# A hybrid decoder trunk: the dilated mixer's second score product on all 128 rows of the array

## The chip, the cores and the metric

One NeuronCore of a Trainium2 chip runs the whole program. The metric is the time on the device of one execution, in microseconds (us), as the median of the runs.

## What is computed

Two layers of a decoder over 1024 tokens of 1024 columns. Each layer projects the tokens to the inputs of four causal mixers of four heads each (A: differential attention, B: spatial gating, C: a dilated mixture, D: an mLSTM), projects the four outputs back, adds and normalizes, and ends with a gated feed-forward. The change is in mixer C. The reference takes three attentions with the same q, k and v, that differ in the keys that a query may see, and mixes them by their softmax sums:

```
def dilated_mixture(q, k, v):
    outs, lses = [], []
    for window, dilation in DILATED_PATTERNS:
        o, l = dilated_pattern(q, k, v, window, dilation)
...
    wts = jax.nn.softmax(jnp.stack(lses, 0), axis=0)
```

This is one softmax over all earlier keys, with a mask that counts by how many of the three patterns a key is seen, and the kernel computes it so: scores q·k over 64 columns a head, plus the mask, exponential, sum, and a product with the values.

## The kernel before

**Split numbers.** The products of the projections and of the scores take operands of the type fp32r, which holds a part of an fp32 number. So each operand is a high part, rounded to fp32r, and a low part, the rest. A projection adds three products (high·high, high·low, low·high) into one PSUM bank (`proj_tok`).

**The stacks of mixer C** (`stacks`, kind "C"). A head has 64 columns, the array of TensorE 128 rows. Per pair of heads, q and k are transposed and written into the arena RA from column `R_ST` on. For q, one block of 512 columns a head: rows 0 to 63 hold q's high part, rows 64 to 127 its low part. For k, two blocks of 1024 columns a head: the first has k's high part in rows 0 to 63 (ScalarE, L415) and again in rows 64 to 127 (GpSimd, `dup`, L421); the second has k's low part in rows 0 to 63 (VectorE, L416), and its rows 64 to 127 are not used.

**The scores** (`attn_S`). A tile is 128 queries of one head, numbered i = 0 to 7; it needs i+1 blocks of 128 keys, in one chunk of keys for i below 4 and in two above. For each chunk a first product of all 128 rows gives q-high·k-high + q-low·k-high, and a second one, of 64 rows, adds q-high·k-low:

```
self.mm(bank[:, 0:wm], self.r(q, 128), self.r(kk + c0, wm), True, False)
self.mm(bank[:, 0:wm], self.r(q, 128, 0, 64), self.r(kk + 1024 + c0, wm, 0, 64), False, True)
```

Chunks have 256, 384 or 512 columns. Four heads of twelve chunks make 48 second products a layer, 96 in the program. VectorE then adds the mask and takes the extreme (L512), ScalarE the exponential (L517).

**The order on TensorE** is the order in which the program is written. `step` interleaves, by the strings `C1` (i below 4) and `C2` of `ORDER`, the scores of this tile (S, one chunk each), the transposes of the weights of the tile two steps earlier (T), their product with the values (P), the end of an earlier pair of tiles (t), and pieces of a queue of projections (- and .), which `Fill` hands out:

```
'C1': 'TT.S-.PP-t', 'C2': 'STT-S--PP-t'
```

So the second product is followed at once by two transposes in the first chunk of tiles 4 to 7 (16 a layer, 32 in all), and by a projection's product otherwise (64 in all). P waits for ScalarE's copy of the transposed weights out of PSUM (`attn_T`, L229). Between a pair's stacks and its first scores some 9 us of projections are issued (`STACK`). The other engines' instructions are ordered by a scheduler. GpSimd computes, in its own order, the low parts of the projections' weights (L256), the copies of k's high part (L421), and small steps of the norms.

**The same arena holds mixer A's stacks** before: four blocks of 1024 columns for k and four of 512 for q, with 96 rows each. Mixer C's low parts lie where A's second and fourth block of keys were.

Of the kernel before, what the change touches and what calls it, by code (L numbers as in the profile page):

```python
# [9 lines left out]
F32 = mybir.dt.float32  # L10
# [5 lines left out]
S = 1024  # L16
D = 1024
# [8 lines left out]
# fp32r arena, in floats per partition  # L26
R_T = 0
R_W = 16384
R_ST = R_W + 6144
R_SIZE = 28672  # L30
# fp32 arena
# [18 lines left out]
# the last slot of q|k is followed by room for the mLSTM values' window of 128 columns  # L50
# [3 lines left out]
# flexible area: fp32 while the mixers run  # L54
# [10 lines left out]
# mLSTM, after the attentions  # L65
# [5 lines left out]
# slots of the weights: 0..5 and 16..23 in the fp32r arena, 6.. in tiles of their own  # L71
DOWN_SLOTS = [[0, 1, 2, 3, 4, 5, 16, 17], [18, 19, 20, 21, 22, 23, 6, 7], [2, 3, 4, 5, 6, 7]]
# where the seven left factors of the Strassen-Winograd products live in the fp32r arena
# [10 lines left out]
# steps of the attention. S: scores of a chunk of keys, T: transposition, P: product with the values,  # L84
# t: end of a pair of tiles, - and .: products from the queue
# [16 lines left out]
class Fill:  # L102
    """a queue of products that are issued between the steps of a chain of dependent work"""
# [28 lines left out]
def blend(a, start, b, every):  # L132
    """work a, with a piece of b after every few of its pieces from a given one on"""
    for i, d in enumerate(a):
        yield d
        if i >= start and (i - start) % every == 0:
            yield next(b, 0.0)
    yield from b


class Trunk:
# [119 lines left out]
    def wplan(self, units):  # L261
        """the weights of the mixers in the order of their use, through three slots"""
        self.wq = collections.deque(units)
        self.wready = collections.deque()
        self.wslots = collections.deque()
# [11 lines left out]
    def rstd(self, out, var, n):  # L277
        """out = (var + eps) ** -0.5 on [128, n]"""
        nc = self.nc
        nc.gpsimd.tensor_scalar(out, var, EPS, 1.0, ALU.add, ALU.mult)  # L280
        nc.gpsimd.tensor_tensor(out, out, self.f(C_MH, 1).to_broadcast([128, n]), ALU.pow)

# [1 line left out]
    def make_T(self, t, src):  # L284
        """src [128 tokens, 1024] fp32 of token tile t into the T ring."""
        h, c = divmod(t, 4)
        for g in range(2):
            bank = self.tr_bank()
            b3 = bank.rearrange("p (k n) -> p k n", k=4)
            for k in range(4):  # L290
                self.tp(b3[:, k, :], src[:, (4 * g + k) * 128:(4 * g + k + 1) * 128])
            self.split(self.th(h)[:, 4 * g:4 * g + 4, c * 128:(c + 1) * 128],
                       self.tl(h)[:, 4 * g:4 * g + 4, c * 128:(c + 1) * 128], b3)

    def behind(self, ins, other):
        """issue order on an engine: ins after other"""
        self.tc.add_manual_dep(ins.ins, other.ins.name,
                               mybir.DependencyInfo(mybir.DependencyClass.NoSync, mybir.DependencyReason.DATA),
                               reason="later")

# [1 line left out]
    def proj_tok(self, kss, n, evac, per_bank=2):  # L302
        """z[:, cols] in token layout. kss: the k blocks of each weight unit; evac(t, bank)"""
        units = []
        for ks in kss:
            hi, lo, slot = self.wready.popleft()
            hi, lo = (w[:, 0:len(ks) * n].rearrange("p (k n) -> p k n", k=len(ks)) for w in (hi, lo))
            units.append((hi, lo, slot, ks))
        for t0 in range(0, 8, per_bank):
            bank = self.mm_bank()  # L310
            for tt in range(per_bank):
                t = t0 + tt
                h, c = divmod(t, 4)
                out = bank[:, tt * n:(tt + 1) * n]
                for hi, lo, slot, ks in units:
                    for i, k in enumerate(ks):
                        xh = self.th(h)[:, k, c * 128:(c + 1) * 128]
                        xl = self.tl(h)[:, k, c * 128:(c + 1) * 128]
                        self.mm(out, xh, hi[:, i, :], k == 0, False)
                        yield n * MM  # L320
                        self.mm(out, xh, lo[:, i, :], False, False)
                        yield n * MM
                        self.mm(out, xl, hi[:, i, :], False, k == 7)
                        if k == 7 and tt == per_bank - 1:
                            evac(t0, bank)
                        if t == 7 and i == len(ks) - 1:
                            self.wdone(slot)
                        yield n * MM
# [4 lines left out]
    def proj_qk(self, slot, ng, hd, cos_off):  # L333
        """q|k of two heads with rope; ng groups of hd columns; half = hd // 8"""
        nc = self.nc
# [22 lines left out]
    def proj_v(self, v):  # L358
        """v: [128, 8 tiles, 256] fp32"""

        def evac(t0, bank):
            self.copy(v[:, t0:t0 + 2, :], bank.rearrange("p (t c) -> p t c", t=2))
            self.vdone = t0 + 2

        return self.proj256(evac)

# [1 line left out]
    def stacks_A(self, src, dst, lo_first, late):  # L368
        """src: callable tile -> [128, 128] (4 maps x 32) ; dst: list of 4 [96, 512] stacks"""
# [19 lines left out]
    def stacks(self, kind, slot, what, half, late=False):  # L389
        """q or k of two heads, transposed, hi and lo parts stacked along the contraction"""  # L390
# [35 lines left out]
    def attention(self, kind, v, col0, slots, marks):  # L426
        """all four heads; marks: what to do at the start of a pair of heads, before a given step"""
        self.steps = 0
        for hp in range(2):
# [45 lines left out]
    def attn_S(self, T):  # L475
# [20 lines left out]
        for m in range(nmap):  # L496
            for ci, (c0, wd) in enumerate(chunks):
# [6 lines left out]
                else:  # L504
# [3 lines left out]
                    self.mm(bank[:, 0:wm], self.r(q, 128, 0, 64), self.r(kk + 1024 + c0, wm, 0, 64), False, True)  # L508
# [18 lines left out]
    def attn_T(self, T):  # L527
        """the weights, transposed"""
# [13 lines left out]
    def attn_PV(self, T):  # L542
        """even key blocks into the rows 0..63, odd ones into 64..127; two query tiles to a bank"""
# [49 lines left out]
    def norm_A(self):  # L593
        """RMS norm of A's outputs, per head"""
# [67 lines left out]
    def proj_dqk(self, l):  # L662
        """q and k: transposed projection, causal depthwise convolution, 2 * silu"""
# [35 lines left out]
    def proj_do(self):  # L699
        """tanh of half the output gate"""  # L700
        ot = self.x(X_OT, 2048).rearrange("p (n c) -> p n c", n=8)
        self.gated = 0

        def evac(t0, bank):
            self.nc.scalar.activation(ot[:, t0:t0 + 2], bank.rearrange("p (t c) -> p t c", t=2), AF.Tanh, scale=0.5)
            self.gated = t0 + 2

        return self.proj256(evac)

    def proj_dv(self):  # L710
        """values and gates of the mLSTM"""
# [13 lines left out]
    def gates_D(self, l):  # L725
        """the gates' logs, running maxima and factors"""
# [42 lines left out]
        # running maximum over the chunks, on one partition  # L769
# [29 lines left out]
        # rows to all partitions through DRAM  # L799
# [11 lines left out]
    def mixer_D2(self, l, c):  # L811
        """recurrence over the chunks; a generator that leaves the tensor engine to other work"""
# [95 lines left out]
    def D_out(self, n0, H):  # L908
        """LayerNorm over the 64 columns of each head, output gate; H [128, 2, 4, 64]"""
# [25 lines left out]
    def make_T_pair(self, t0, ks):  # L935
        """two k blocks of two adjacent token tiles into the T ring"""
# [10 lines left out]
    def mixed_T(self):  # L947
        """outputs of A, B and C, from DRAM, transposed"""
# [40 lines left out]
    def out_part(self, tt, units, ks):  # L989
        """512 columns of a token tile; units: weights of two k blocks each, from block ks[0]"""  # L990
# [11 lines left out]
    def out_A(self, xsrc):  # L1002
        """first half of the columns; A, B and C of six tiles, before the mLSTM ends"""
# [12 lines left out]
    def out_B(self, xsrc, unit):  # L1016
        """the rest of the first half of the columns"""
# [19 lines left out]
    def out_C(self, l):  # L1037
        """second half, first norm (its gain and bias join in after the transposition), start of gate and up"""
# [27 lines left out]
        # the first products, which need the first half of the tokens only, while the last tiles are made  # L1066
# [16 lines left out]
    def form(self, tt):  # L1083
        """left factors of a token tile; those that take both halves of the tokens, after its second tile"""
# [3 lines left out]
        # tiles that have been transposed, or staging, hold what is being mixed  # L1088
# [41 lines left out]
    # ---- feed-forward: gate and up, by Strassen-Winograd over token halves, halves of the contraction  # L1130
    # and gate|up ----
# [11 lines left out]
    def f1_head(self, l, i):  # L1143
        """the right factors of the first two products of tile i"""
# [8 lines left out]
    def f1_prep(self, l, i):  # L1153
        """the right factors of tile i"""
# [70 lines left out]
    def f1_last(self, i):  # L1225
        """the same in an order that frees the mixed left factors first"""
# [352 lines left out]
```

## Time and profile before

| | |
|---|---|
| median of 3 runs | 2654.44 us (2653.58 to 2655.23) |
| span of the profiled execution | 2633.2 us, from its first to its last instruction |
| around the span (launch and end), median less span | 21.2 us |
| TensorE's products, share of the span | 97% |
| weight loads of TensorE | 80% |
| VectorE, ScalarE, GpSimd | 61%, 38%, 18% |
| mean granted clock of TensorE | 0.992 |
| mixer C, layer 1 and layer 2 | about 206 to 360 us and 1512 to 1666 us |

The profile gives the profiled execution by its span alone; the table's third line is worked out with the median of the runs, and so is not known for that one execution. A product on TensorE is a weight load (PEld) and a MATMUL (PE); a row such as `64*128 64x512` means 64 rows by 128 columns of the array in use, and 512 columns streamed through it. Ends of products are modelled, starts are measured. Times on the right of a bar are the idle time of the engine just before, with what ended it.

### The profile page before, as it was taken

The numbers are of one execution on the slowest core, as the hardware profiler recorded it, in microseconds if no ns is written. First come the engines' busy times: TensorE is split into PE (matmuls) and PEld (weight loads), VectorE is DVE, ScalarE is ACT, GpSimd is POOL, SyncE is SP. The second block draws the span as 40 slices with busy tenths as digits, with TensorE's granted clock in tenths as the row PEclk, the third lists the DMA queues.
The fourth block names the chain that finished last, engine by engine and source line by source line (L and its number), as shares of the span: only waits on it lengthen the run. The fifth ranks groups of instructions, "written<-read, shape, count | busy, mean of one in ns | idle before, by whom it ended". The sixth has DMA issues, their size and how long they took to land. (4 is left out here: it accounts for less than half of the span.)

```text
span 2633.2 us, 36905 instructions
## 1 busy us (share of the span) xinstructions
PE 2560.7 (97%) x14128; PEld 2110.0 (80%) x14128; DVE 1601.7 (61%) x3219; ACT 1004.0 (38%) x1918; POOL 484.7 (18%) x478
## 2 busy tenths in 40 slices
PE   8999998998999999999999999989989999999998
PEld 8988886776888888788899878877868888887886
DVE  4775346768766665632756743467687666656336
ACT  4675553226333333211246755522353333322110
POOL 2214122115000000600221231211230000007002
PEclk9999999999999999999999999999999999999999
DMA  4112112412222222532321111132122222235322
GB/s 159 50 36 68 35 34 79 141 54 104 105 80 76 84 81 87 176 120 68 116 76 52 46 56 34 55 121 89 66 103 93 84 80 76 85 104 176 96 84 76
DMA packets 120673, 224.24 MB, mean 85 GB/s; under 512 B 16816, under 2 KB 67888, under 8 KB 120496
## 3 DMA queue, kind: packets, MB, share of 16 engines
q1 hardware_dynamic: 107792, 179.93, 20.9%
q0 software_dynamic: 12704, 41.95, 4.2%
q8 instruction: 111, 1.82, 0.3%
q14 instruction: 66, 0.54, 0.1%
HBM read 167.77 MB, written 46.20 MB: 81 GB/s over the span
## 5 line engine op out<-in xcount | busy, mean ns | idle before, releaser
L222 PE MATMUL bank<-RA 128*128 128x256 f32 (+7 forms) x5016 | 851.6, 317 | 13.8 <-ACT XA L229 9.7
L222 PE MATMUL bank<-RA,wb 128*128 128x512 f32 x3600 | 845.6, 397 | 11.0 <-ACT wb L234 7.4
L222 PEld LDWEIGHTS bank<-RA,wb 128*128 128x128 f32 x3600 | 679.4, 189 | 177.2 <-ACT wb L234 8.3
L222 PEld LDWEIGHTS bank<-RA 128*128 128x128 f32 (+2 forms) x5016 | 696.4, 192 | 107.3 <-issue 44.6
L222 PE MATMUL bank<-RA,h 128*128 128x512 f32 x1728 | 412.8, 396 | 6.3 <-DVE RA L235 5.7
L222 PEld LDWEIGHTS bank<-RA,h 128*128 128x128 f32 x1728 | 323.3, 188 | 87.1 <-DVE RA L235 7.5
L234 ACT ACTIVATE wb<-FA 128x512 fp32r<-128x512 f32 x300 | 189.2, 635 | 500.0 <-PE bank L222 480.3
L235 DVE TENSOR_TENSOR wb<-FA,wb 128x512 fp32r<-128x512 f32 x300 | 208.4, 699 | 5.5 <-ACT wb L234 3.4
L256 POOL TENSOR_TENSOR RA<-FA,RA 128x512 fp32r<-128x512 f32 (+2 forms) x112 | 145.5, 1318 | 325.3 <-ACT RA L255 317.5
L512 DVE CUSTOM_DVE_ANT_0 XA<-bank,XA 128x384 f32<-128x384 f32 (+2 forms) x192 | 109.7, 572 | 128.2 <-PE bank L222 126.6
L517 ACT ACTIVATE XA<-XA,FA 128x128 f32<-128x128 f32 (+3 forms) x192 | 148.4, 773 | 55.3 <-DVE FA L512 54.2
L235 DVE TENSOR_TENSOR RA<-FA,RA 128x1024 fp32r<-128x1024 f32 (+2 forms) x64 | 92.6, 1464 | 95.0 <-ACT RA L234 93.9
L1221 POOL DMA_DIRECT2D hid<-FA x44 | 23.8, 541 | 671.9 <-DVE FA L1212 640.5
L1322 DVE TENSOR_TENSOR FA<-FA,bank 128x512 f32<-128x512 f32 x96 | 64.2, 684 | 136.7 <-PE bank L222 136.7
L234 ACT ACTIVATE RA<-FA 128x512 fp32r<-128x512 f32 (+2 forms) x96 | 78.3, 826 | 168.6 <-DMA FA<-in_w_down 119.6
L225 PE MATMUL bank<-FA,XA 128*128 128x128 f32 (+2 forms) x824 | 128.4, 274 | 6.2 <-DVE XA L929 3.2
L229 ACT ACTIVATE XA<-bank 128x512 f32<-128x512 f32 (+5 forms) x228 | 103.6, 484 | 79.7 <-PE bank L225 66.2
L225 PEld LDWEIGHTS bank<-FA,XA 128*128 128x128 f32 (+2 forms) x824 | 91.4, 140 | 32.8 <-issue 7.8
L234 ACT ACTIVATE h<-FA 128x1024 fp32r<-128x1024 f32 (+1 forms) x48 | 46.9, 988 | 172.1 <-PE bank L222 144.0
L280 POOL TENSOR_SCALAR FA<-FA 128x1 f32<-128x1 f32 (+1 forms) x48 | 17.9, 372 | 504.4 <-DVE FA L976 350.7
L222 PE MATMUL bank<-wx,RA 128*128 128x512 f32 x384 | 97.7, 406 | 0.0
L222 PE MATMUL bank<-XA 128*64 128x128 f32 (+1 forms) x836 | 92.2, 291 | 3.4 <-DVE XA L749 2.5
(187 smaller groups left out, 2647.8 us busy)
## 6 DMA issues: line engine op xcount, KB each, us to landing
FA<-in_w_in SPq DMA_DIRECT2D x44, 512.0 KB, 3.7
FA<-in_w_gate SPq DMA_DIRECT2D x44, 512.0 KB, 3.3
FA<-in_w_up SPq DMA_DIRECT2D x44, 512.0 KB, 3.2
hid<-FA POOLq DMA_DIRECT2D x88, 256.0 KB, 2.3
FA<-in_w_down SPq DMA_DIRECT2D x44, 512.0 KB, 3.3
FA<-hid SPq DMA_DIRECT2D x32, 512.0 KB, 4.0
x<-FA POOLq DMA_DIRECT2D x24, 512.0 KB, 3.0
FA<-x SPq DMA_DIRECT2D x24, 512.0 KB, 4.2
```

Source lines behind the costliest of these rows:

```text
L222: self.nc.tensor.matmul(out, lhsT=lhsT, rhs=rhs, start=start, stop=stop)
L225: self.nc.tensor.transpose(out, src, self.FA[0:p, C_ID:C_ID + p])
L229: self.nc.scalar.activation(out, src, AF.Copy)
L234: self.nc.scalar.activation(hi, src, AF.Copy)
L235: (self.nc.gpsimd if pool else self.nc.vector).tensor_tensor(lo, src, hi.bitcast(F32), ALU.subtract)
L256: nc.gpsimd.tensor_tensor(lo[:, c], raw[:, c], hi[:, c].bitcast(F32), ALU.subtract)
L280: nc.gpsimd.tensor_scalar(out, var, EPS, 1.0, ALU.add, ALU.mult)
L512: nc.vector.tensor_tensor_reduce(sv[m][:, c0:c0 + wd], bank[:, 0:wd], mask[:, off:off + wd], -scale, init, ALU.add, ALU.min, acc)
L517: self.last_exp = nc.scalar.activation(sv[m][:, 0:n], sv[m][:, 0:n], AF.Exp, bias=nb[:, m:m + 1], scale=-1.0, accum_out=den[:, m:m + 1])
L1221: nc.gpsimd.dma_start(self.scr["h"][i, 0], v)
L1322: nc.vector.tensor_tensor(xc, xc, banks[2 * q + ch], ALU.add)
```

## The change

The rows 64 to 127 of the two blocks of k's low parts are set to zero once a layer, at the start of mixer C, by two GpSimd instructions of 64 x 1024. The second product then takes all 128 rows of the same q block as the first: q-high meets k-low, and q-low meets zeros. The sum is the same. Comments were taken out of the file as well, and line numbers from L428 on are higher by 5.

```diff
     def attention(self, kind, v, col0, slots, marks):
-        """all four heads; marks: what to do at the start of a pair of heads, before a given step"""
+
+        nc = self.nc
         self.steps = 0
+        if kind == "C":
+
+            for m in range(2):
+                nc.gpsimd.memset(self.r(R_ST + m * 2048 + 1024, 1024, 64, 128).bitcast(F32), 0.0)
         for hp in range(2):
...
                     self.mm(bank[:, 0:wm], self.r(q, 128), self.r(kk + c0, wm), True, False)
-                    self.mm(bank[:, 0:wm], self.r(q, 128, 0, 64), self.r(kk + 1024 + c0, wm, 0, 64), False, True)
+                    self.mm(bank[:, 0:wm], self.r(q, 128), self.r(kk + 1024 + c0, wm), False, True)
```

TensorE, VectorE, ScalarE and the DMA queue of SyncE keep all their instructions in the same order, and the number of products and of weight loads is the same. GpSimd gets two instructions more a layer. At the turn from mixer A to mixer C of layer 1, GpSimd's order was (L256: low parts of the projections' weights; L421 64x512: the copies of k's high part for C's first pair of heads; L421 32x512: such copies for A):

```order
L421 TENSOR_SCALAR RA<-FA 32x512 x6
L256 TENSOR_TENSOR RA<-FA,RA 128x512 x4
L421 TENSOR_SCALAR RA<-RA 64x512 x2
L256 TENSOR_TENSOR RA<-FA,RA 128x512 x4
L421 TENSOR_SCALAR RA<-RA 64x512 x2
```

and is now:

```order
L421 TENSOR_SCALAR RA<-FA 32x512 x6
L256 TENSOR_TENSOR RA<-FA,RA 128x512 x4
L433 MEMSET RA 64x1024 x2
L421 TENSOR_SCALAR RA<-RA 64x512 x2
L256 TENSOR_TENSOR RA<-FA,RA 128x512 x4
L421 TENSOR_SCALAR RA<-RA 64x512 x2
```

Nothing else has moved there: the two zeroings stand right ahead of the copies of k's high part, and in layer 2 they stand at the same place between the same rows. The first zeroing waits for the last scores of mixer A that read the second block of keys, the other for the last that read the fourth, which are the last scores of A.

## Rows read from the trace of the kernel before

**Rows 1.** The page: TensorE's busy time, and its granted clock in 40 slices

```profile
PE 2560.7 (97%) x14128; PEld 2110.0 (80%) x14128; DVE 1601.7 (61%) x3219; ACT 1004.0 (38%) x1918; POOL 484.7 (18%) x478
...
PEclk9999999999999999999999999999999999999999
```

**Rows 2.** Busy time by window: mixer C of layer 1, its first pair's tiles 0 to 3

```profile
core 0: us, PE busy (x) PEld busy (x) DVE busy (x) ACT busy (x) POOL busy (x), PEclk, DMA share, GB/s
...
206.00:360.00 154.00, 153.56 (x1134) 121.89 (x1133) 58.75 (x195) 81.62 (x197) 37.06 (x43) 1.00 0.13 42
...
217.00:232.80 15.80, 15.80 (x102) 11.11 (x100) 11.23 (x37) 10.72 (x32) 8.46 (x10) 1.00 0.11 39
```

**Rows 3.** Waits of TensorE, 206 to 360 us: total us, times, longest

```profile
PE bank L222 <- ACT XA L229: 0.4, 1, 0.4
```

**Rows 4.** Second score products of 512 and 256 columns: busy us, mean ns, idle before

```profile
L222 PE MATMUL bank<-RA 64*128 64x512 f32 x40 | 19.7, 494 | 0.0
...
L222 PE MATMUL bank<-RA 64*128 64x256 f32 x32 | 12.2, 381 | 0.0
```

**Rows 5.** Weight loads of 96 rows (scores of A) and 64 rows (second products)

```profile
L222 PEld LDWEIGHTS bank<-RA 96*128 96x128 f32 x192 | 36.2, 189 | 7.5 <-issue 4.8 <-DVE FA L512 1.8
...
L222 PEld LDWEIGHTS bank<-RA 64*128 64x128 f32 x96 | 17.5, 183 | 18.7 <-issue 14.4
```

**Rows 6.** Timeline of TensorE, tile 3: first product, second product, a projection's; start, us

```profile
300.00 0.40 PE L222 MATMUL bank<-RA 128*128 128x512 f32 x1
...
300.32 0.49 PE L222 MATMUL bank<-RA 64*128 64x512 f32 x1
...
300.75 0.38 PE L222 MATMUL bank<-RA 128*128 128x256 f32 x1
```

**Rows 7.** Timeline of TensorE: dense 512 columns, projections, transposes; one transpose alone

```profile
1002.82 7.39 PE L222 MATMUL bank<-RA,wb 128*128 128x512 f32 x31
...
277.70 10.43 PE L222 MATMUL bank<-RA 128*128 128x256 f32 x85
...
287.97 0.82 PE L225 MATMUL bank<-FA,XA 128*128 128x128 f32 x6
...
299.76 0.27 PE L225 MATMUL bank<-FA,XA 128*128 128x128 f32 x1
```

**Rows 8.** Timeline of TensorE, first chunk of tile 6: first, second product, first transpose

```profile
250.91 0.50 PE L222 MATMUL bank<-RA 128*128 128x512 f32 x1
...
251.34 0.49 PE L222 MATMUL bank<-RA 64*128 64x512 f32 x1
...
251.76 0.33 PE L225 MATMUL bank<-FA,XA 128*128 128x128 f32 x1
```

**Rows 9.** Timeline of ScalarE and TensorE: copies of weights, and the products that wait

```profile
222.99 0.49 ACT L229 ACTIVATE XA<-bank 128x384 f32<-128x384 f32 x1
...
223.55 0.65 PE L222 MATMUL bank<-XA 128*64 128x128 f32 x6
...
306.06 0.60 ACT L229 ACTIVATE XA<-bank 128x512 f32<-128x512 f32 x1
...
306.99 0.55 PE L222 MATMUL bank<-XA 128*64 128x128 f32 x6
```

**Rows 10.** Timeline of TensorE and GpSimd at the turn from A to C, layer 1

```profile
195.77 0.50 PE L222 MATMUL bank<-RA 96*128 96x512 f32 x1
...
199.11 1.48 POOL L421 TENSOR_SCALAR RA<-RA 64x512 fp32r<-64x512 f32 x1 [36.27 <-ACT RA L415]
...
203.12 5.05 POOL L256 TENSOR_TENSOR RA<-FA,RA 128x512 fp32r<-128x512 f32 x4 [1.09 <-issue]
```

**Rows 11.** Instructions of GpSimd: a zeroing, a copy (min/median/max ns), a two-input step

```profile
L716 POOL MEMSET FA<- 128x64 f32 x2 | 0.3, 151 | 9.5 <-PE bank L222 9.2 <-POOLq L1569 0.3
...
L421 POOL TENSOR_SCALAR RA<-RA x16: 611/613/1476, 199.1 to 1604.0; 64x512 fp32r<-64x512 f32 x16
...
L1303 POOL TENSOR_TENSOR FA<-FA,LNP 128x1024 f32<-128x1024 f32 x16 | 47.7, 3005 | 11.9 <-issue 11.9
```

## The prediction

> **What bounds the kernel now.** I read the page first, then the table of windows over mixer C, the list of waits there, the groups by form, and the timeline around single scores. The page puts TensorE at 97% of the span with a granted clock of nine tenths or more of full speed in every slice [rows 1]; no other engine is above 61%. In mixer C it is tighter still: 153.56 of 154.00 us, while ScalarE has 81.62 and VectorE 58.75 [rows 2], and TensorE's only wait that the trace lists there is one of 0.4 us, for a copy of ScalarE [rows 3]. So mixer C lasts as long as TensorE's own products last, in the order in which they are written, and what a product loses inside the array is lost from the run.
>
> The groups by form show a product that loses time. The 96 second products of the scores take 494 ns for 512 columns and 381 for 256 [rows 4], where a first product of 512 takes 400 ns [rows 6]. Their weight load itself is as quick as others (183 ns against 189), but before 96 such loads the loader stood idle for 18.7 us, 195 ns each; before the 192 loads of 96 rows in mixer A it was 7.5 us, 39 ns each [rows 5]. So a part-filled array is no trouble as such, but one of 64 rows is: its load is not brought forward under the product before it.
>
> **What one 64-row product costs.** I measure from the end of the first product to the end of the product after the second, which leaves out the latency that every product has. In rows 6 the first product ends at 300.00 + 0.40 = 300.40 and the projection's product at 300.75 + 0.38 = 301.13: 0.73 us. In a dense stretch a product of 512 columns takes (7.39 - 0.40) / 30 = 0.233 us and one of a projection 10.43 / 85 = 0.123 [rows 7], together 0.356. So 0.37 us is lost at such a place. Where transposes follow, the first product ends at 251.41 and the first transpose at 251.76 + 0.33 = 252.09, 0.68 us apart [rows 8]; dense, this is 0.233 and, for a transpose, (0.82 - 0.27) / 5 = 0.11, with 0.27 for one alone [rows 7]. So 0.34 us is lost there. The loss does not hang on the width: for 256 columns the second product's duration is 381 ns, 113 less than for 512, and the dense prices of the two differ by as much, 0.233 - 0.123 = 0.11. I take the same loss for all widths.
>
> **The sum.** Of the 96 second products 32 are followed by transposes and 64 by a projection (by the order strings). 64 x 0.37 + 32 x 0.34 = 23.7 + 10.9 = 34.6 us of TensorE's time go, if a 128-row second product costs what other 128-row products cost. Above, it is bounded by a price by columns alone: the two dense prices differ by 0.11 us for 256 columns, so 512 would cost 0.22 instead of 0.233 and 256 would cost 0.11 instead of 0.123; 96 x 0.013 = 1.2 us more, 35.8 us. Below, by the dearest neighbour: the first products that follow 64-row transposes last 0.50 instead of 0.40 us [rows 8, 6]; if every second product came 0.10 later, 25.0 us would be left. I take 34.6, since a second product follows a 128-row product with the very same q block, the situation of a projection's high·high and high·low products.
>
> **What is late next.** P waits for ScalarE's copy of the transposed weights, and the score between T and P was part of its cover. In six tiles a layer the copy is ready less than 0.4 us before P: the first of them is done at 223.48 for a P that starts at 223.55, the last at 306.66 for 306.99 [rows 9]; the six slacks are 0.07, 0.05, 0.39, 0.31, 0.05 and 0.33 us. With 0.37 taken out, 0.30 + 0.32 + 0 + 0.06 + 0.32 + 0.04 = 1.0 us a layer becomes a wait, 2.1 us in all. In the other tiles the slack is above 0.5 us. That leaves 34.6 - 2.1 = 32.5 us.
>
> **The zeroing** costs GpSimd two instructions a layer. The trace has none of that size. Nearest from below: a zeroing of 64 columns takes 0.15 us, from above: a two-input step on 1024 columns takes 3.0 us [rows 11]; a one-input pass over 512 columns of 64 rows takes 0.61, so I take 1.2 us each. The second may start when A's last score is done, at 195.77 + 0.50 = 196.3; GpSimd idles then, for 36.27 us up to 199.11, when its copy of k's high part gets ScalarE's data [rows 10]. At 1.2 us the zeroing ends at 197.5 and delays nothing. At 3.0 us it ends at 199.3, 0.2 us late, and the low parts of the weights that follow at 203.12 have 1.09 us of idle time before them [rows 10]. If that cover were gone, 1.2 us a layer would be added to the copies, and TensorE still has some 9 us of projections between the stacks and the first scores. I cost it at nothing, at most 0.4 us in all. The loads of the weights for the second product stay as many, and of the same length. No DMA is added.
>
> The sum is made against the profiled execution's span of 2633.2 us, which goes to 2600.7; the runs' median stands 21.2 us above that span, and with the same 21.2 the time is 2654.4 - 32.5 = **2621.9 us**.
>
> **Rivals.**
>
> *ScalarE becomes the bound in tiles 0 to 3.* These have one chunk each, so a step is short while ScalarE has exponential, copies, splits of weights, and in the first pair of heads the squares of A's norm. Over 217 to 232.8 us it is busy 10.72 of 15.80 us [rows 2]; with the six second products in it 0.37 us shorter each, that is 10.72 of 13.6, from 68% to 79%. If all that the 32 products of these tiles give is lost to waits (32 x 0.37 = 11.8 us, of which 2.1 are in the sum already), 34.6 - 11.8 = 22.8 us are left: 2631.6 us. For it speaks that two P's there have no slack at all; against it, that over all of mixer C ScalarE has half the time free.
>
> *Rows do not matter to a product's time.* The idle time before the loads could come from reading another stretch of q, or from a second product in the same bank, rather than from the 64 rows. Then the change moves nothing: 2654.4 us. The Trainium skill says, in "TensorE: Matmul & The Clock Gate", section "Why this matters for your kernels", that a single product with 32 rows of contraction takes the same time as one with 128; by that rule the sum would be zero. Against it: rows 4 and 6 show 494 and 400 ns for the same 512 columns, and rows 5 show the idle time at 64 rows and not at 96. By the trace the rule fails here. The same bank is no cause either, since the projections add their products into one bank at 0.123 us each [rows 7].
>
> *GpSimd holds mixer C up: slower than before.* The zeroing stands ahead of the copies of k's high part, for which the first scores wait, and of the weights' low parts. Place: GpSimd from 196.3 us on. It costs TensorE nothing until it ends after about 199, and from then on, less the 1.09 us of idle time, each us of it delays the weights' low parts and soon TensorE as much. To eat the 16.2 us that a layer gains it would have to last to about 199 + 1 + 16 = 216 us, 10 us for each zeroing. If it took that and half as much again, 15 us each, the end would be 226 and the time 2654 + 2 x 10 = 2674 us. Against it: 3.0 us is the longest that GpSimd needs for twice the rows and two inputs [rows 11].
>
> **How the numbers follow.** The forecast has 0.84, ScalarE as the bound 0.10, no effect 0.05, GpSimd in the way 0.01. The predicted time is the forecast's. Its own bounds are 35.8 and 25.0 us, that is 2618.6 and 2629.4 with no new wait. Two readings of a hundredth of a us stand behind each loss, 96 x 0.02 = 1.9 us, so the range is **2616.5 to 2629.5**. It leaves out the rivals, and with 0.16 between them no more than the 2 in 10 that may be left. A measurement of this kernel can tell about 0.2%, 5 us, from no change. Forecast and first rival are both beyond that: faster 0.94; the second is no change, 0.05; slower 0.01.
>
> **What would show it.** Right: the 96 second products appear as 128*128, at about 400 ns for 512 columns, and no weight load of 64 rows is left in RA; the distance in rows 6 shrinks from 0.73 to about 0.36 us; mixer C's stretch goes from 154 to some 138 us a layer; TensorE's waits for the copies grow from 0.4 to 1 to 2 us a layer; L433 lasts about 1.2 us and lies in GpSimd's idle stretch. Wrong: products of 128 rows that still start 0.4 us apart (the switch is not what costs), or waits of many us for ScalarE (the bound has moved), or a late L421 at the turn from A to C.

## The result, and the profile after

The changed kernel takes **0.9876** of the time before, 95% interval 0.9857 to 0.9895, from six executions of each; their medians are 2612.41 and 2654.01 us. The two medians alone would give 0.984; the executions of the kernel before lie apart (four at 2653.58 to 2656.55 us, two at 2641.2), and the result is read by the ratio with its interval. On the 2654.44 us of the table it is 2621.5 us (2616.5 to 2626.6), where 2621.9 was predicted. It is faster, by 1.2%.

The page of the changed kernel, the lines that answer to [rows 1]:

```profile
span 2604.3 us, 36911 instructions
...
PE 2528.6 (97%) x14128; PEld 2108.1 (81%) x14128; DVE 1603.1 (62%) x3219; ACT 1003.4 (39%) x1918; POOL 486.7 (19%) x482
```

TensorE has as many products as before and is busy 32.1 us less (2560.7 to 2528.6); GpSimd has four instructions more. TensorE is the bound as before, at 97%.

The windows that hold the same work as [rows 2], layer 1 and layer 2 (length, busy time of PE, PEld, DVE, ACT, POOL, granted clock, DMA share, GB/s):

```profile
206.00:343.50 137.50, 135.96 (x1133) 119.94 (x1133) 58.08 (x195) 81.47 (x197) 36.45 (x43) 1.00 0.15 47
1495.70:1633.20 137.50, 135.97 (x1131) 119.94 (x1132) 58.04 (x194) 81.48 (x197) 36.75 (x43) 1.00 0.15 47
```

Mixer C goes from 154.0 to 137.5 us in each layer; the weight loads, VectorE and ScalarE have the same work. TensorE is idle for 1.54 us of it instead of 0.44. Its waits there, 206 to 343.5 us (total us, times, longest), against [rows 3]:

```profile
PE bank L222 <- ACT XA L229: 1.4, 3, 0.8
```

The forms of the score products and loads, by busy us, mean ns, and idle time before, against [rows 4, 5]. The second products have joined the first ones, so the counts are larger:

```profile
L222 PE MATMUL bank<-RA 128*128 128x512 f32 x872 | 220.3, 401 | 4.2 <-POOL RA L256 2.3 <-DVE FA L662 2.0
...
L222 PE MATMUL bank<-RA 128*128 128x384 f32 x48 | 12.4, 338 | 0.0
```

```profile
L222 PEld LDWEIGHTS bank<-RA 128*128 128x128 f32 x4824 | 673.6, 192 | 72.4 <-issue 18.7 <-ACT XA L229 9.3 <-POOL RA L256 4.2
...
L222 PEld LDWEIGHTS bank<-RA 96*128 96x128 f32 x192 | 36.2, 189 | 7.5 <-issue 4.8 <-DVE FA L517 1.9
```

No product or load of 64 rows is left in RA. The busy time of the loads hardly moves; what went is the idle time before them.

The same three products of tile 3 as in [rows 6] (start us, us), and the first chunk of tile 6 as in [rows 8]:

```profile
290.80 0.40 PE L222 MATMUL bank<-RA 128*128 128x512 f32 x1
...
291.04 0.40 PE L222 MATMUL bank<-RA 128*128 128x512 f32 x1
...
291.27 0.39 PE L222 MATMUL bank<-RA 128*128 128x256 f32 x2
```

```profile
246.51 0.51 PE L222 MATMUL bank<-RA 128*128 128x512 f32 x1
...
246.85 0.39 PE L222 MATMUL bank<-RA 128*128 128x512 f32 x1
...
247.08 0.49 PE L225 MATMUL bank<-FA,XA 128*128 128x128 f32 x3
```

In tile 3 the first product ends at 290.80 + 0.40 = 291.20. The third row holds the projection's product and the next, and the first of the two ends at 291.54 (it lasts 0.27 us in the trace): 0.34 us apart, where it was 0.73. The second product there takes 0.40 us, was 0.49, and starts 0.24 us after the first, was 0.32. In tile 6 the first of the three transposes ends at 247.35 (it lasts 0.27 us in the trace), 0.33 us behind the first product, where it was 0.68.

GpSimd at the turn from A to C, against [rows 10]:

```profile
177.01 0.95 POOL L433 MEMSET RA<- 64x1024 f32 x1 [14.17 <-issue]
196.31 0.96 POOL L433 MEMSET RA<- 64x1024 f32 x1 [18.36 <-PE bank L222]
199.02 1.55 POOL L421 TENSOR_SCALAR RA<-RA 64x512 fp32r<-64x512 f32 x1 [1.76 <-ACT RA L415]
...
202.75 5.04 POOL L256 TENSOR_TENSOR RA<-FA,RA 128x512 fp32r<-128x512 f32 x4 [0.74 <-POOL RA L421]
```

Each zeroing takes 0.95 us in an idle stretch, and the copies of k's high part still wait for ScalarE (L415), not for the zeroing.

**Where the time went.** TensorE issues the same products in the same order, so product number k of one trace can be set against number k of the other. Before mixer C the two run level. Over mixer C of layer 1 the changed kernel gains 16.45 us, between the mixers next to nothing (0.2 us are given back), over mixer C of layer 2 another 16.48: 32.9 us for the two mixers. Behind it, in the rest of layer 2, some 4 us are given back, so the two profiled spans differ by 28.9 us (2633.2 and 2604.3). The 4 us are taken up with the last experiment below.

### The profile page after: what moved, and what is told of

The parts are those of the page before. It is cut to its first block, busy times and chain, and to the rows that moved or that the text cites. A ratio compares the mean times of both kernels' runs of the same rounds, so it can differ in the third digit from the quotient of the medians.

```text
span 2604.3 us, 36911 instructions
## 1 busy us (share of the span) xinstructions
PE 2528.6 (97%) x14128; PEld 2108.1 (81%) x14128; DVE 1603.1 (62%) x3219; ACT 1003.4 (39%) x1918; POOL 486.7 (19%) x482
## 5 line engine op out<-in xcount | busy, mean ns | idle before, releaser
L222 PE MATMUL bank<-RA 128*128 128x256 f32 (+6 forms) x5016 | 820.9, 314 | 14.2 <-ACT XA L229 8.4
L222 PEld LDWEIGHTS bank<-RA 128*128 128x128 f32 (+1 forms) x5016 | 690.2, 192 | 79.9 <-issue 23.5
L256 POOL TENSOR_TENSOR RA<-FA,RA 128x512 fp32r<-128x512 f32 (+2 forms) x112 | 143.7, 1303 | 322.0 <-ACT RA L255 315.4
L517 DVE CUSTOM_DVE_ANT_0 XA<-bank,XA 128x384 f32<-128x384 f32 (+2 forms) x192 | 109.6, 571 | 110.0 <-PE bank L222 108.7
L225 PE MATMUL bank<-FA,XA 128*128 128x128 f32 (+2 forms) x824 | 126.5, 272 | 7.4 <-DVE XA L934 3.2
```

What stands on the lines that cost most here:

```text
L222: self.nc.tensor.matmul(out, lhsT=lhsT, rhs=rhs, start=start, stop=stop)
L225: self.nc.tensor.transpose(out, src, self.FA[0:p, C_ID:C_ID + p])
L256: nc.gpsimd.tensor_tensor(lo[:, c], raw[:, c], hi[:, c].bitcast(F32), ALU.subtract)
L517: nc.vector.tensor_tensor_reduce(sv[m][:, c0:c0 + wd], bank[:, 0:wd], mask[:, off:off + wd], -scale, init, ALU.add, ALU.min, acc)
```

## The experiments

The theory: a 64-row product among 128-row ones costs TensorE about 0.37 us, whatever its width, because the array is switched from work on 128 rows to work on 64 and back, and this is what the change saves. The rivals: the saving comes with the zeroing or with reading one q block twice; each idle row has a price; ScalarE or GpSimd takes part of it back. The measure is the length of mixer C, from the start of the first mask step to the start of the last (VectorE's mask line, L512 before, L517 in the changed kernel). Unlike the time of a whole execution it repeats to 0.2 us. Before, the steps of layer 1 start from 209.4 to 355.0, 145.6 us apart, and those of layer 2 from 1515.7 to 1661.3, as far apart:

```profile
L512 DVE CUSTOM_DVE_ANT_0 XA<-bank,XA x32: 290/624/694, 209.4 to 353.1; 128x512 f32<-128x512 f32 x16, 128x384 f32<-128x384 f32 x8, 128x128 f32<-128x128 f32 x4, 128x256 f32<-128x256 f32 x4
L512 DVE CUSTOM_DVE_ANT_0 XA<-bank,XA,FA x16: 482/551/751, 239.3 to 355.0; 128x256 f32<-128x256 f32 x8, 128x384 f32<-128x384 f32 x4, 128x512 f32<-128x512 f32 x4
```

In the changed kernel the steps run from 209.2 to 338.7, 129.5 us, and in layer 2 from 1499.2 to 1628.8:

```profile
L517 DVE CUSTOM_DVE_ANT_0 XA<-bank,XA x32: 271/616/694, 209.2 to 337.1; 128x512 f32<-128x512 f32 x16, 128x384 f32<-128x384 f32 x8, 128x128 f32<-128x128 f32 x4, 128x256 f32<-128x256 f32 x4
L517 DVE CUSTOM_DVE_ANT_0 XA<-bank,XA,FA x16: 475/551/752, 236.7 to 338.7; 128x256 f32<-128x256 f32 x8, 128x384 f32<-128x384 f32 x4, 128x512 f32<-128x512 f32 x4
```

### The zeroing alone

The two zeroings stay, the second product goes back to 64 rows:

```diff
-                    self.mm(bank[:, 0:wm], self.r(q, 128), self.r(kk + 1024 + c0, wm), False, True)
+                    self.mm(bank[:, 0:wm], self.r(q, 128, 0, 64), self.r(kk + 1024 + c0, wm, 0, 64), False, True)
```

> The zeroing of the change, with the second products left at 64 rows. Measure: mixer C's length, from the start of the first mask step on its scores to the start of the last, 145.6 us in either layer of the kernel before and 129.5 in the changed one. Theory (a 64-row product costs a switch of the array's rows, and the zeroing is hidden in idle time of GpSimd): 145.6 within 0.3 in both layers. Rival (the gain comes with the zeroing, say from another place of GpSimd's work): 129.5, or anything in between.

Mixer C took 145.6 us (209.8 to 355.4) in layer 1 and as long in layer 2, the length before. One execution took 2639.75 us, in the range of the kernel before on that chip (2636.73 to 2653.57). The loads of 64 rows stand idle as before, to the tenth:

```profile
L222 PEld LDWEIGHTS bank<-RA 64*128 64x128 f32 x96 | 17.5, 183 | 18.7 <-issue 14.4
```

So the zeroing by itself neither costs nor gains anything that shows; the 16 us a layer come with the rows of the second product.

### 96 rows instead of 128

The second product takes rows 0 to 95, and only rows 64 to 95 are zeroed. It then reads other rows of the q block than the first product, and leaves a quarter of the array unused:

```diff
-                nc.gpsimd.memset(self.r(R_ST + m * 2048 + 1024, 1024, 64, 128).bitcast(F32), 0.0)
+                nc.gpsimd.memset(self.r(R_ST + m * 2048 + 1024, 1024, 64, 96).bitcast(F32), 0.0)
...
-                    self.mm(bank[:, 0:wm], self.r(q, 128), self.r(kk + 1024 + c0, wm), False, True)
+                    self.mm(bank[:, 0:wm], self.r(q, 128, 0, 96), self.r(kk + 1024 + c0, wm, 0, 96), False, True)
```

> The second product takes 96 rows, and only rows 64 to 95 are zeroed. Theory (what costs is the array split for 64 rows; 96 rows take the whole array, as mixer A's scores do): the same as with 128 rows, mixer C's length 129.5 us in either layer, ratio to the kernel before about 0.988. Rival 1 (each row left out costs its part): half of the gain, 137.6 us. Rival 2 (the gain at 128 rows comes from loading the very same q block twice in a row): none of the gain, 145.6 us, since 96 rows are another block.

Mixer C took 129.8 us in both layers, here 207.5 to 337.3 in layer 1:

```profile
L517 DVE CUSTOM_DVE_ANT_0 XA<-bank,XA x32: 271/615/692, 207.5 to 335.7; 128x512 f32<-128x512 f32 x16, 128x384 f32<-128x384 f32 x8, 128x128 f32<-128x128 f32 x4, 128x256 f32<-128x256 f32 x4
L517 DVE CUSTOM_DVE_ANT_0 XA<-bank,XA,FA x16: 476/551/752, 235.0 to 337.3; 128x256 f32<-128x256 f32 x8, 128x384 f32<-128x384 f32 x4, 128x512 f32<-128x512 f32 x4
```

The ratio is 0.9874 (0.9838 to 0.991), that of the change. Weight loads of 96 rows are now three for every two before, with the same idle time in all:

```profile
L222 PEld LDWEIGHTS bank<-RA 96*128 96x128 f32 x288 | 54.4, 189 | 7.5 <-issue 4.8 <-DVE FA L517 1.8
```

So it is not that unused rows cost by the row, nor that both products read the very same q block. 64 rows among 128 cost time; 96 among 128 do not.

### Two 64-row stretches put side by side

The kernel before, with the pair's end (t, two 64-row transposes) moved right behind the second chunk's 64-row product in tiles 4 to 7. No product changes its rows; only the changes between 64 and 128 rows are fewer:

```diff
-'C2': 'STT-S--PP-t'
+'C2': 'STT-St--PP-'
```

> The kernel before, second products at 64 rows; in tiles 4 to 7 the end of an earlier pair, two transposes of 64 rows, is issued right behind the second chunk's second product instead of at the end of the step. It does so at 8 places a layer, so 8 stretches of 64 rows less. Theory (the switch costs, not the product): 8 x 0.37 = 3.0 us less a layer, mixer C's length 142.6 us, unless the pair's data is late there. Rival (a 64-row product is slow by itself, whatever stands beside it): 145.6 us or more.

Mixer C took 142.9 us in both layers, 2.7 us less than before, with 142.6 expected; one execution took 2633.55 us. In layer 1 (209.89 to 352.75 in times of two decimals):

```profile
L512 DVE CUSTOM_DVE_ANT_0 XA<-bank,XA x32: 290/611/693, 209.9 to 350.8; 128x512 f32<-128x512 f32 x16, 128x384 f32<-128x384 f32 x8, 128x128 f32<-128x128 f32 x4, 128x256 f32<-128x256 f32 x4
L512 DVE CUSTOM_DVE_ANT_0 XA<-bank,XA,FA x16: 474/550/751, 239.8 to 352.7; 128x256 f32<-128x256 f32 x8, 128x384 f32<-128x384 f32 x4, 128x512 f32<-128x512 f32 x4
```

The second products still take their 494 ns at 512 columns:

```profile
L222 PE MATMUL bank<-RA 64*128 64x512 f32 x40 | 19.8, 494 | 0.0
```

The 64-row products last as long, and yet 2.7 us went where eight stretches a layer were joined to neighbours: 0.34 us for each. And at the 16 joined places the trace has no idle time before the load of the first transpose, of 64 rows like the product ahead of it, while 128-row loads behind a 64-row product wait 0.18 to 0.23 us. So the price hangs on the change of rows, once for a stretch of 64-row work, not on the product.

### Only the places before transposes

The change in the first chunks of tiles 4 to 7 alone, 16 products a layer:

```diff
+                    rows = 128 if ci == 0 and len(chunks) == 2 else 64
...
+                    self.mm(bank[:, 0:wm], self.r(q, 128, 0, rows), self.r(kk + 1024 + c0, wm, 0, rows), False, True)
```

> Of the change only the second products of the first chunk of tiles 4 to 7 (16 a layer, those with transposes behind them); the other 32 stay at 64 rows. Theory by the terms of the prediction: 16 x 0.34 = 5.4 us a layer, no new wait, mixer C's length 140.2 us. If a place with transposes gave as much as one with a projection: 139.7. If the gain were in the tiles 0 to 3 or in the second chunks alone: 145.6.

Mixer C took 140.1 us in both layers, where 140.2 was expected: 5.5 us less than before, which is 16 x 0.344. One execution took 2635.23 us. The loads left at 64 rows, two thirds of the 96, have 11.3 of the 18.7 us of idle time left:

```profile
L222 PEld LDWEIGHTS bank<-RA 64*128 64x128 f32 x64 | 11.7, 183 | 11.3 <-issue 7.0
```

So these 16 places gain by themselves what they gain in the whole change; the gains of places add up.

### GpSimd's slack

The second zeroing eight times, to load GpSimd with 6.7 us more a layer ahead of the copies:

```diff
-            for m in range(2):
+            for m in (0, 1, 1, 1, 1, 1, 1, 1, 1):
```

> The change, with the second zeroing of each layer, the one that cannot start before A's last score, done eight times instead of once (0.95 us each in the changed kernel's profile, so 7.6 us in place of 0.95). Measure: TensorE's time from A's last score to the first mask step of mixer C, 195.8 to 209.2 us in the changed kernel, and mixer C's length, 129.5 us. Theory (GpSimd costs nothing until the copies of k's high part come late, and then nearly one for one): the zeroing ends at 196.3 + 7.6 = 203.9 instead of 197.3, the first copy starts 4.9 us late, the low parts of the weights some 3 us late; with about 0.5 to 1 us of slack TensorE waits 2 to 3 us a layer before the first scores, and mixer C's length stays 129.5. Rival (it holds up nothing, there are 9 us of projections in front): no change. Rival (every us counts): 6.7 us a layer.

This expectation missed. Mixer C stayed at 129.5 us in both layers, and its start moved little: from the start of A's last score to C's first mask step it is 14.0 us instead of 13.4, some 0.5 us a layer. The timeline of GpSimd says why: the scheduler did not leave the zeroings in one block, but spread them between the copies and the weights' low parts:

```profile
197.33 2.97 POOL L433 MEMSET RA<- 64x1024 f32 x3 [18.36 <-PE bank L222]
200.28 1.31 POOL L421 TENSOR_SCALAR RA<-RA 64x512 fp32r<-64x512 f32 x1
201.54 1.95 POOL L433 MEMSET RA<- 64x1024 f32 x2
203.47 0.62 POOL L421 TENSOR_SCALAR RA<-RA 64x512 fp32r<-64x512 f32 x1
...
211.26 0.95 POOL L433 MEMSET RA<- 64x1024 f32 x1
```

TensorE's wait for GpSimd there, 196 to 212 us:

```profile
PE bank L222 <- POOL RA L256: 0.3, 1, 0.3
```

The experiment as meant, a late block ahead of the first copy, was therefore not made. What it shows is that 6.7 us more on GpSimd at this turn cost TensorE half a us, so that the 1.9 us of the change are far from mattering. (Its time, 2624.08 us, holds a wait of 11.5 us in the last feed-forward, which one execution of the unaltered change also shows; see the end of this section.)

### Other 64-row stretches: the ends of pairs

If the switch is what costs, the pair's end of two 64-row transposes pays it too, 64 times in mixers A and C. Here they too are of 128 rows, with zeros below, written once a layer ahead of mixer A (64 x 512, 0.52 us on GpSimd):

```diff
+        pair["oT128"] = self.x(X_WK + 256 + (self.pvp % 2) * 256, 256)
...
-            self.tp(bank[:, q * 64:(q + 1) * 64], P["oT"][:, q * 128:(q + 1) * 128], 64)
+                self.tp(bank[:, q * 128:(q + 1) * 128], P["oT128"][:, q * 128:(q + 1) * 128], 128)
...
+        nc.gpsimd.memset(self.x(X_WK + 256, 512, 64, 128), 0.0)
```

> The change, and the other 64-row stretches of the two attentions at 128 rows too: the two transposes at the end of each pair of tiles, 64 in the program's mixers A and C, take 128 rows, the lower half zeros that are written once a layer, and so 128 columns instead of 64. In the changed kernel's trace such a pair of transposes with the projection's product behind it takes 0.58 us; dense, two transposes of 128 columns and that product take 0.11 + 0.11 + 0.12 = 0.34. Theory (the switch of rows costs wherever it stands): 64 x 0.2 to 0.24 = 13 to 15 us less than the change, mixer C's length 126 us in place of 129.5 (16 pairs a layer), ratio to the kernel before about 0.982. Rival (transposes are not hurt by the switch, they only get longer): 64 x 2 x 0.03 to 0.05 = 4 to 6 us more than the change.

Mixer C took 126.5 us in both layers, 3.0 less than with the change alone; mixer A, by the same measure, went from 142.8 to 139.8, and the profiled span is 13.3 us under that of the changed kernel (2591.0). That is 0.19 us of the mixer's length for each of its 16 pairs, where 0.2 to 0.24 was expected. The ratio to the kernel before is **0.9825** (0.9797 to 0.9854). Five executions of the change in the same set gave 0.9858 (0.9832 to 0.9884). The intervals of the two overlap; that this version is the faster one rests on the traces and on the medians, 2602.04 and 2607.65 us. The 0.19 us a pair are less than the 0.34 of a joined stretch; the transposes move 128 columns now instead of 64, and that takes part of the gain back. Their forms before the edit (the changed kernel) and after:

```profile
L225 PE MATMUL bank<-FA,XA 128*128 128x128 f32 x688 | 104.7, 276 | 7.1 <-DVE XA L934 3.2 <-DMA XA<-mixed 3.1 <-DVE XA L527 0.8
...
L225 PE MATMUL bank<-FA,XA 64*128 64x64 f32 x128 | 21.4, 247 | 0.0
```

```profile
L225 PE MATMUL bank<-FA,XA 128*128 128x128 f32 x816 | 125.4, 275 | 6.9 <-DVE XA L941 3.0 <-DMA XA<-mixed 2.9 <-DVE XA L527 0.8
```

On top of this, another order in tiles 0 to 3: the full piece of projections (-) goes between the transposes and the score and the half piece (.) behind P, to give ScalarE's copies more cover:

```diff
-'C1': 'TT.S-.PP-t'
+'C1': 'TT-S-.PP.t'
```

> As the one before, and in tiles 0 to 3 of mixer C half a gap of projections' work more between the transposes and the product with the values, taken from behind it (order TT-S-.PP.t in place of TT.S-.PP-t). Theory (the change's new waits, 1.4 us a layer, come from the copy that is not ready at that product): the waits fall by 0.5 to 1 us a layer, 1 to 2 us less in all. Rival (ScalarE is the bound in these tiles, and the wait only moves): no difference.

Mixer C took 126.4 and 126.6 us, and TensorE waited 1.5 and 1.7 us for the copies, against 1.8 and 1.1 without the order, where 0.5 to 1 us less a layer was expected:

```profile
PE bank L222 <- ACT XA L229: 1.5, 3, 0.7
...
PE bank L222 <- ACT XA L229: 1.7, 4, 0.7
```

The expectation missed: the wait moves and does not go. The ratio, 0.9808 (0.9781 to 0.9836), cannot be told from that of the version without it.

64-row products are left in mixer D: 256 of them (XA, 64 rows by 128 columns), in 80 stretches. No run changed those.

### Where 4 us went behind mixer C

In the first pair of profiles the gain shrinks from 32.9 to 28.9 us behind mixer C of layer 2; 3 us of it sit at one place. The windows show the clock there, in the changed kernel and in the kernel before at the same products (length, busy of PE, PEld, DVE, ACT, POOL, granted clock, DMA, GB/s):

```profile
1778.50:1785.30 6.80, 6.80 (x25) 4.92 (x24) 2.50 (x11) 0.00 (x0) 0.00 (x0) 0.50 0.25 62
```

```profile
1811.00:1818.00 7.00, 7.00 (x43) 5.29 (x43) 4.97 (x18) 0.63 (x1) 0.00 (x0) 1.00 0.18 58
```

The granted clock is 0.50 for 6.8 us, that is 1.2 instead of 2.4 GHz, and 25 products take the time of some 43. In the 13 us ahead of the fall TensorE was busy for 11.52 us at the full clock:

```profile
1765.00:1778.00 13.00, 11.52 (x80) 9.23 (x78) 11.42 (x26) 4.99 (x9) 7.37 (x6) 1.00 0.52 190
```

To see whether the change brings this on, both kernels were run again, twice each, with no edit.

> The changed kernel once more, beside the others on one chip. Theory: mixer C's length 129.5 us in both layers; ratio 0.986 to 0.989; and behind mixer C of layer 2 the 3 us that the first profile gave back there come and go with the times at which the granted clock falls, so that they are here or not, as they were in the run with the zeroing alone. Rival (the change itself costs 3 us behind mixer C in layer 2): the same 3 us at the same place.

> The kernel before, profiled once more. The trace of the changed kernel showed a fall of the granted clock of 6.8 us behind mixer C of layer 2, 70 us into what follows it, that the first trace of the kernel before does not have; it costs 3 us. Theory (falls of the clock in the mixers' thin stretches come or go from one execution to the next, whatever the kernel): in one of two more traces of the kernel before it is there. Rival (the change brings it): in neither. In both, mixer C's length is 145.6 us in either layer, and the time lies within 3 us of the span.

> As the run before it: the kernel before, a third trace, for the same two theories on the falls of the clock behind mixer C of layer 2.

> The changed kernel, a third trace. Theory: mixer C's length 129.5 us in either layer, whatever the falls of the clock do elsewhere; and at least once in three traces the fall behind mixer C of layer 2 is at another place or missing. Rival (the change brings it): at the same place again.

The length of mixer C repeated: 129.5 us in both layers in each run of the change, 145.6 us in the runs of the kernel before. The fall of the clock came at this place in all three traces of the change, and in one of three of the kernel before, as this row, of a repeated execution of it, shows:

```profile
1812.00:1820.00 8.00, 8.00 (x29) 5.89 (x29) 3.90 (x14) 0.07 (x1) 0.00 (x0) 0.57 0.22 60
```

It also came with the zeroing alone, whose products are those of the kernel before. So the change is not needed for it; but the expectation that a third trace of the change would have it elsewhere, or not at all, missed. The traces of the other experiments have the same place too: all seven traces without a 64-row second product show the fall there (three of the change, and those of 96 rows, of the eightfold zeroing and of both versions with the pairs' ends), and so do three of the six with such products (one of three of the kernel before, the zeroing alone, the first chunks alone; not the joined stretches). That points to the change making it more frequent, but the traces are few and no run shows why; it stays open. Where it comes it takes 3 us.

The last of these runs has another wait, in layer 2's last feed-forward, where the first trace of the changed kernel has 2.9 us:

```profile
PE bank L222 <- DVE RA L235: 11.5, 1, 11.5
```

It lies 750 us behind mixer C, and a wait of this kind is enough to make single executions differ by 10 us. The granted clock is another part of their scatter: of the 19 executions of the kernel before that were made beside the experiments, the quickest (2636.62 us) has a mean granted clock of 0.991, the slowest (2656.23 us) one of 0.985.

## Why the prediction was right

- **TensorE bounds mixer C**, and what a product loses there is lost from the run: shown. A layer's mixer C is 16.5 us shorter, and no other engine has moved in.
- **The price of a 64-row product.** Of the 96 places, measured as in the prediction over all of them, 64 with a projection behind give back 0.389 us each and 32 with transposes 0.344: 64 x 0.389 + 32 x 0.344 = 35.9 us, where 34.6 was predicted with 0.37 and 0.34. Each of these was read off a single place, in times of two decimals. With a projection behind and 512 columns, the distance before is 0.738 us where 0.73 was read, and after the change it is 0.350 where 0.356 was put. It does not hang on the width, as assumed: 0.388 us for 256 columns, 0.391 for 384, 0.388 for 512.
- **Why it is lost** was put down to the load of the 64-row product, which is not brought forward. That is half of it: in the kernel before, the load behind it, of 128 rows, stood idle as long, as tile 3 of [rows 6] shows (start us, us); over all 96 places it is 0.195 us before the one and 0.190 before the other:

```profile
300.32 0.18 PEld L222 LDWEIGHTS bank<-RA 64*128 64x128 f32 x1 [0.25 <-issue]
300.75 0.53 PEld L222 LDWEIGHTS bank<-RA 128*128 128x128 f32 x4 [0.24 <-issue]
```

  So the change is paid for on the way in and on the way back, and the runs show the rest: a stretch of 64-row work pays once (joined stretches of up to three products), and 96 rows pay nothing. That the array takes another form for 64 rows is how this is read; no row names the form that it is in. The Trainium skill, "TensorEngine Tiling (Array Packing)", lists forms of 128, 64 and 32 rows in the section "Available Configurations", and says in "Key Properties" that a change of the mode drains TensorE. The traces agree, with joined stretches paying once and a loader that stands idle at both ends, and put the price here at 0.34 to 0.39 us a stretch.
- **The lower bound**, 25.0 us, took the 0.50 us of the first products behind 64-row transposes as what a second product might cost. No second product became so slow: they take 0.39 to 0.40 us at 512 columns.
- **New waits** were put at 1.0 us a layer, by the slacks of six tiles. The trace lists 1.4 us instead of 0.4, in three waits of up to 0.8 us and not in six of up to 0.32, and together with smaller delays that it doesn't list 35.9 - 32.9 = 3.0 us of the two layers are given back, where 2.1 was predicted. So the net, 32.9 us, was met within 0.4 by two errors of opposite sign, 1.3 and 0.9 us: that closeness is luck.
- **The zeroing** takes 0.95 us each instead of 1.2 and delays nothing, as predicted; alone it changes nothing.
- **The rivals.** ScalarE as the bound would have left 22.8 us; the windows of mixer C give 33. That rows do not matter, as the Trainium skill has it for a product taken by itself ("TensorE: Matmul & The Clock Gate", section "Why this matters for your kernels"), does not carry over to a 64-row product among 128-row ones: 494 ns before and 392 to 398 after for the same 512 columns, and nothing lost at 96 rows. GpSimd in the way is ruled out by the turn from A to C, and had half a us to show for 6.7 us more work. Its price had both zeroings start behind 196.3 us; the first ran at 177.01, so the second alone would have had to fill the 20 us.
- **One step was wrong without effect.** The 21.2 us "around the span" are not there: the executions whose span is known have some 2 us around it (2606.07 less 2604.3 is 1.8). The profiled execution of the kernel before was simply quicker than the median; the other executions of this kernel took 2636.6 to 2656.6 us. As the same 21.2 stood on both sides, the difference was not touched.
- **The range** was not worked out evenly. From the bounds 2618.6 and 2629.4 it takes the 1.9 us of reading off the lower one, but does not add them, or the 2.1 us of new waits, to the upper one, which would be 2633.4. The measured time lies in the middle, so this had no effect.
- **The spans alone** differ by 28.9 us, less than the net of mixer C, since the one fall of the clock and smaller delays behind it fell into the changed kernel's trace. The ratio of many executions, 32.9 us (28 to 38), is what the sum is to be held against. The second set of five executions gave 0.9858, that is 37.7 us (31 to 45). So no time of whole executions confirms the sum to better than some 5 us; the lengths of mixer C do.

## What to carry to other kernels

Look in the groups by form for products that use 64 rows of the array between products that use 128, and measure from the end of the one before to the end of the one after: here each stretch cost 0.34 to 0.39 us. Padding with zeros to 96 or 128 rows removed it here with no price on TensorE, where the number of columns stayed the same (the transposes, whose columns doubled, gave 0.19 us a pair). Where padding isn't possible, putting such products side by side pays once for the stretch. When executions scatter by ten us, compare the length of the changed stretch in the trace, which repeated to 0.2 us here, and not the spans.

## What was not expected of the hardware

- 64 rows are special, 96 are not: idle time of 195 ns before each load of 64 rows, 39 ns and less at 96.
- The transposes at the ends of pairs, 64 x 64, cost TensorE less at four times the size: 128 x 128 with zeros saved 3.0 us of each mixer C, at 16 pairs a mixer.
- The granted clock fell to half, for 3.4 to 10.6 us at a time, 8 to 13 times in each of the thirteen traces. Most falls come at the same places of the program in all of them; some, as the one behind mixer C of layer 2, come in some executions and not in others.
